# Eight leading matmuls, the cross-attention's output product in seven block products, and an issue order written as a table

## The chip, the core and the metric

The kernel runs on one core of one Trainium2 chip. The number that counts is the device time of one execution in microseconds (us), as a median of several runs. Five engines work side by side on a core, each through its own queue in order: TensorE (PE in the profile; its weight loads are PEld), VectorE (DVE), ScalarE (ACT), GpSimd (POOL) and SyncE (SP), which here issues most of the DMA transfers.

## What is computed

Two encoder layers over 512 positions of width 1024, all in float32. Each has a mixing part (differential attention beside a recurrent branch), a cross-attention into 256 memory tokens, and an MLP; every part ends in a matrix product that is added to the residual `x`. Cut to what matters here:

```
for l in range(DEPTH):                              # DEPTH = 2
    h = rms_norm(x, g_mix[l]);  z = h @ w_in[l]
    ...                                             # attention o, recurrent branch r
    x = x + concatenate([o, r]) @ w_out[l]
    hq = rms_norm(x, g_xq[l])
    qx = (hq @ xa_wq[l]).reshape(B, S, X_HEADS, X_HEAD_DIM)     # 4 heads of 256
    ...
    p = softmax(einsum('bshd,bmhd->bhsm', qx, kx) * X_HEAD_DIM ** -0.5)
    ox = einsum('bhsm,bmhd->bshd', p, vx).reshape(B, S, D_MODEL)
    x = x + ox @ xa_wo[l]                           # the product that is changed
    hm = rms_norm(x, g_mlp[l])
    x = x + square(relu(hm @ mlp_w1[l])) @ mlp_w2[l]
return rms_norm(x, g_final)
```

## The kernel before

**Layout and precision.** `x` lies transposed: eight chunks `c_x` of 128 channels by 512 positions. To keep float32 accuracy every operand of a product is split into a rounded part and a rest (`hi` and `lo`, by one ScalarE copy and one VectorE subtraction), and each product is three matmuls: hi by hi, hi by lo, lo by hi. A weight tile is 128 by 1024 floats, so 512 KB: SyncE loads it into `wraw` (three buffers), ScalarE makes `whi`, VectorE `wlo` (three buffers each). In the profile all work of the program has one line, L490, since one helper (`emit`) issues it; groups are told apart by tile names: `b` is any 128 by 512 work tile, `mm` (three) and `at` (five) are PSUM banks, `s` small columns, `pt` the transposed attention probabilities and some scratch.

**The order.** `trunk` writes the whole program down as operations in a `Plan` (`record`); `schedule` then places them by an estimate of each one's duration, due times and a string of corrections (`LEADS`), and `emit` issues them in that order. So what stands behind what on an engine is fixed when the program is built.

**The start.** GpSimd fills constants, among them `c_ones` and the identity. SyncE and ScalarE load parameters, `x` and the first weights, in halves. ScalarE and VectorE split the first chunk and the first weight half, and then TensorE begins `v_products`: 96 matmuls of 512 columns, chunk after chunk. A small product of `c_ones` (`lam_col`) stands in front of them.

**The cross-attention's end.** For each of four heads (`XHead`): scores, softmax, transposition (`turn`), and `pv`, which makes two tiles of 128 by 512 and splits each in hi and lo (list `ox`, eight tiles). Then `residual_fm` is called eight times a layer: `gemm_fm` multiplies one weight tile with the eight chunks (24 matmuls of 128 by 128 by 512), and VectorE adds the result to `x[c]`. `prep_x` scales and splits the new chunk for the MLP.

**The MLP's second product** is already done otherwise. `left_pair` turns two neighbouring tiles into the seven left operands of a 2 by 2 block product in seven multiplications, `right_pair` turns two weight tiles into the seven right operands, and `seven` does the seven products. Each product is 12 matmuls of 256 columns, and its bank is added to the residual in one or two pieces of 128 by 256.

Of the kernel before, what the change touches and what calls it, by code (L numbers as in the profile page):

```python
# [11 lines left out]
F32 = mybir.dt.float32  # L12
# [6 lines left out]
P = 128  # L19
# [30 lines left out]
ATT_AHEAD = 3  # L50
SPLIT_AHEAD = 18.0
LOAD_AHEAD = 105.0
CAST_AHEAD = 28.0
NEG_AHEAD = 20.0
DMA_T = (1, 4, 13, 36, 51)


LEAD_STEPS = '#$%&()*+,-./0123456789:;<=>?@ABCDEFGHIJKLMNOPQRSTUVWXYZ[]^_`abcdefghijklmnopqrstu'
LEADS = (
    'uL63BCuGGgGGGG@@<<HGuue>d>auFOMu9Q-ZAAGA-2D-H)?NNOC*@%AD?EA#6&/,0,?CBBB,=5>BBDFA?1J1C-G;JF$80?FUFKP;'  # L60
    'eOD?AK9NLPBWOOZ``Y[S^YcRURQTTRQNPLNNNTJJPIJJLISQR[XMMXXOGHOJFMMABIQPVUkUU[[[WTPSSLLJLuuLRSCNRJJJKJEG'
    'GVSXQNMECF>lK`LLJIJIKKNK```KCDDIDcCjL[YSeY_Ua0^NGLLGGLIGP>LEU@@D@0L4HHKKPutukM<=tYfYfBKOPKuuuu[uTZuK'
    'JOOHTtmqtmufuuFCVbmuDDM7MRLCZrruuu0&u?;;;K6CDC4uuuuuuCuuuuMussuguuuuKIDQa>OEYC;>X@<EgqlsultlllutluPQ'
    'QVV:Wqo^^ZQQF25BGIuuuuuuuuuuNZknIBNEKiWuuuuuuuuuutuusGGA:LJGN_quU_lYYYVuuuuuubuuuubuuuudsuuu_lonEbab'
    'QkdkGWhmmS^E_aetGFV`UmiusL7U1UaaUoOJJkVV`N_MJCEEGRFHHHRKFMDLJJKJ@@@MDMJCHDNHHGHHHRGPHKOOHGOHHHVHLAIP'
    'KKKTLTTHHHI6IL>CCRI:RI5JLJV@HPGH;JC;>IGKHDFFCFHFHCFBBBAB@@HIOED_RLLQLEREHEHISTWVTH`VLLJLLMILGLLLMP_^'
    'LLLWUL^LOHJPXLrRWRffVRLPJOOLAPPPNKP_QOFOLOIWFWYMPW]RLRRLLLLLLLLLVLULLULLULLLLLLLLLLVLQSUNLLLELCLILLH'
    'TOOPOO[OOGA@IA@A@KKIKGIKGMIGGILNKJLRPQLLLKKLJLLOLRLLMJLKLLLLLILKKLHHHCH8I8HI8HHHLLI8LLILLLLLLI8LSSSS'
    'SLL8I8L8ILJIJJJLCJLMJLLPLLHLOLLKNLLLLCLALK>LLLLLK<LH>LLLLLK>LLQNN@GQLGKLLNMLQQLPNKKLPJJLKHLVL[LL>RIJ'
    'LLMEOFFGFEW5VU2[VWF$ZZ#W#KG)JDHDFJQ#n]5U^Ru:ufaX`7b2X5pCbGdYQ_RRVAF[Ac[]qsqnoqrPgXHdS=g5LkBTOKGG_?Gu'  # L70
    '<GJIIAbMUASrUMqMb`L`MTMMMMNNNXeZ_ZndVOTTMZMZdeghZZXUMZZZZZZZUUUYUKZSZ[bbbbeeKeJiIK^J]]XUVNQQ=R=IFFJL'
    'LNKKKKWKLJOLLNMLMNLOONNLOLLNNLLONNLLLLOOMONONQLLQMLCLOOOLLSLLMONLONSNLLLLLHLMLFFFILMOLNLFFILNHGLLLLK'
    'LNLMMKLLNLNNLXMLXLLXMLLNLLLMLMXNLLYLLMXLNLMLIXXHLHLLLLHXXHHLIXDLLLLKLLLDUFLQDKQLFELLILCCCFCOEKBBDPEE'
# [12 lines left out]
    'uuutkhbbbusinVTYofODlQ@7lOTGodhkMUjajDTMGgh`JLHZ5QG9m/2:6OR888D;;dZCERCCCEGE@<@:B@:::B@G?>>G>;CCDCCH'
    'G>NPNN@RUTB5B;5?;<;7;;B8;B;8BBFGIAII@>>;><99>>>9>9H?>GGGGGGNMB7D7>ABRMHHOKA?G@GBGJCBNBMBJE=B[NcNcEEd'
    'O?aREEuuuuuuuuWJuu[eH;u;R36Lcm/JHPA?M2Y:IWYt`PPPuPPRQUPPSPVIccicPcce]Rubl[RPHVL@VEXXuuDSluJNKSSQuPPP'
    'NPPSTQ_bnf^WXWRWoJGERPAPBPWL]ZG?QITFGLPHRJcGY]hYWJdNbPUPZgUTf_XZZ_uY[[SZ[u`n_bZHRRJegaXFD[>[=^3_SS1V'
    'LIEiQH-S2$tnneC^ReSNGHH>H7><;THHEHMHHB>P=C@HOFTQDLHeHQdOVUUMMYWY_jQYeeXMMMM_eMMMMMKMKK_bMKKKKaaVVVLQ'  # L90
    'WcWLdLWLSLXNNPPPRQPPP[P_WP[RSP[PE[[[[____GCGPPP[WPWWPPPVVPPRPPD>BCPJWPPOPPPPPCURCO=SXPYSRQIIINIIXV^Q'
    '``SFSPEDAAEELRWTZdMIMNMSSTSOTUOd^WV[XLJLLOLLJ]]ORUUGQFO[MGGGGGGFF*#WaUYa[DSbJLhLoK<UMEKL4UCJa0X/U*%&'
    '[###M###M%%+FOurMuuuruA.mP(S888?=EKHUT_M*MMPLSiuQlaJouuB*=Auuuuuuuuquusu777VAu@qQXWFUXZ.-5=AAEEE???D'
    'T-Z2uuuuuuuuusZZXjTTIHmuumuuuuuIGXGDSAL[Hu`YWURQEHMLHZZ[uuuZuuuuutQuuuuHuouoKuouILS_RJIXYQVV]G^fIPZP'
    'Tu]gXNWuuuuq[agLOmtm;iRULYbe]]]]g[VMOLGUKLNPLOLLLHNLNOOG@WJXLYP`fkGUZHGIPLJLEJJODP@@jluuuuSNchaY^LQE'
    'SIIEAEAOOjJ<<56JCJCBME>8AQTAI<VINOGNLIG[1B83E49>FfNl=>?>?NNDCDLI4QNNIK=EHON0:5=7G^uA5c9UDZAT+=G9GFEG'
    'FEIJJJAOOOL(KMOMP#T;L<L;D:DBM3M@H1*6?9<FiiCJH,GI]cQKZRT`<QLHWV]be_uuuZLRULBBIIQTUSIZWK`LJQQLLEL]IXRI'
# [1465 lines left out]
```

## Time and profile before

| | |
|---|---|
| median of three runs | 1463.85 us (1462.7 to 1465.16) |
| the profiled execution, its own time | 1463.46 us |
| its span in the trace | 1461.7 us |
| TensorE busy | 1430.8 us, 98% of the span |
| VectorE busy | 1108.0 us, 76% |
| ScalarE busy | 758.2 us, 52% |
| chain that ended last | TensorE 82%, VectorE 10%, DMA 3%, ScalarE 3% |

Busy times are unions, so two pipelined matmuls that overlap count once. An engine's share of the whole span says little about one stage; tables by stretch (busy time of each engine between two times, with the number of instructions in it) and the waits of TensorE, with who ended each, say more. For the pace of matmuls the distance from one start to the next is used, not the duration of one, since they overlap.

### The profile page before, as it was taken

Reading aid. Unit: us, or ns where it says so; the run is one execution under the profiler, and the core shown is the slowest. Engines: PE = TensorE matmul, PEld = TensorE weight load, DVE = VectorE, ACT = ScalarE, POOL = GpSimd, SP = SyncE. Lnnn points to the kernel's source line nnn. Section 1 sums busy time; section 2 is a strip of 40 time slices with the busy share of each in tenths; the row PEclk is TensorE's granted clock in tenths of the full one; section 3 lists DMA queues with packets and bytes.
Section 4 is the critical chain, followed back from the end, with each engine's and each line's share of the span. In section 5 each row is a group of like instructions: output and inputs, shape, how many; then the busy total and the mean of one; then the engine's idle time right before and its main releaser. Section 6 shows DMA issues by size and latency. Waiting matters only on the chain.

```text
span 1461.7 us, 20808 instructions
## 1 busy us (share of the span) xinstructions
PE 1430.8 (98%) x8054; PEld 1228.4 (84%) x8054; DVE 1108.0 (76%) x1891; ACT 758.2 (52%) x1164; POOL 41.5 (3%) x69
## 2 busy tenths in 40 slices
PE   8999999999999999999999999999999999999997
PEld 6777887888889889898987779888888898989986
DVE  7889886564679697797958999755655786959786
ACT  6598755443445353444536887644443544435352
POOL 1000000000000000000000011000000000000001
PEclk9999999999999999999999999999999999999998
DMA  6454643221323233233334565422122233232322
GB/s 204 116 144 106 183 159 90 98 72 38 108 87 102 101 102 101 101 102 101 101 115 113 145 167 166 132 87 87 59 71 87 101 102 115 74 115 90 119 81 72
DMA packets 50258, 157.67 MB, mean 108 GB/s; under 512 B 6384, under 2 KB 8560, under 8 KB 50160
## 3 DMA queue, kind: packets, MB, share of 16 engines
q1 hardware_dynamic: 47136, 145.61, 31.1%
q0 software_dynamic: 2880, 10.49, 3.4%
q8 instruction: 63, 1.03, 0.3%
q14 instruction: 35, 0.29, 0.1%
q10 hardware_dynamic: 144, 0.26, 0.0%
HBM read 141.65 MB, written 2.10 MB: 98 GB/s over the span
## 4 chain that ended last, share of the span: by engine, by line
PE 82%; DVE 10%; DMA 3%; ACT 3%; issue 1%; POOL 0%; SPq 0%; DVEq 0%; ACTq 0%; POOLq 0%
PE mm L490 63%; PE at L490 18%; DVE b L490 6%; DVE wlo L490 2%; ACT b L490 1%; DVE s L490 1%; DMA b<-b 1%; DMA wlo<-in_W 1%; ACT whi L490 1%; DVE pt L490 1%; DMA whi<-in_W 1%; DMA wraw<-in_W 0%; ACT L490 0%; POOL s L490 0%; SPq L490 0%
## 5 line engine op out<-in xcount | busy, mean ns | idle before, releaser
L490 PE MATMUL mm<-b,whi 128*128 128x512 f32 (+1 forms) x3640 | 976.4, 356 | 2.5 <-DVE b L490 1.7
L490 PEld LDWEIGHTS mm<-b,whi 128*128 128x128 f32 x3640 | 632.7, 188 | 107.6 <-ACT b L490 3.2
L490 PE MATMUL mm<-b,wlo 128*128 128x512 f32 (+1 forms) x1820 | 645.5, 355 | 1.7 <-DVE wlo L490 1.6
L490 ACT ACTIVATE whi<-wraw 128x1024 fp32r<-128x1024 f32 (+1 forms) x213 | 223.1, 1048 | 346.3 <-PE mm L490 186.8
L490 PEld LDWEIGHTS mm<-b,wlo 128*128 128x128 f32 x1820 | 342.3, 188 | 56.9 <-DVE wlo L490 2.8
L490 DVE TENSOR_TENSOR wlo<-wraw,whi 128x1024 fp32r<-128x1024 f32 (+1 forms) x213 | 257.1, 1208 | 41.3 <-ACT whi L490 40.3
L490 DVE TENSOR_TENSOR b<-b,b 128x512 fp32r<-128x512 f32 (+3 forms) x388 | 223.0, 594 | 10.1 <-ACT b L490 8.6
L490 ACT ACTIVATE b<-b 128x512 fp32r<-128x512 f32 (+2 forms) x288 | 168.8, 602 | 80.7 <-DVE b L490 78.0
L490 DVE SCALAR_TENSOR_TENSOR b<-mm,rb 128x512 f32<-128x512 f32 x80 | 55.2, 690 | 106.5 <-PE mm L490 105.7
L490 DVE TENSOR_TENSOR c_x<-c_x,mm 128x256 f32<-128x256 f32 (+1 forms) x160 | 74.5, 471 | 72.5 <-PE mm L490 71.9
L490 ACT ACTIVATE whi<-pt 128x1024 fp32r<-128x1024 f32 x64 | 67.6, 1060 | 98.9 <-PE mm L490 41.8
L490 PE MATMUL at<-b,whi 128*128 128x256 f32 x520 | 94.6, 278 | 0.0
L490 ACT ACTIVATE b<-at,s 128x512 f32<-128x512 f32 (+2 forms) x100 | 61.1, 615 | 45.6 <-DVE s L490 37.4
L490 PEld LDWEIGHTS at<-b,whi 128*128 128x128 f32 x520 | 79.6, 188 | 0.9
L490 DVE TENSOR_TENSOR wlo<-pt,whi 128x1024 fp32r<-128x1024 f32 x64 | 77.9, 1221 | 2.9 <-ACT whi L490 2.7
L490 PE MATMUL at<-b,wlo 128*128 128x256 f32 x260 | 72.4, 278 | 0.1
L490 PE MATMUL at<-b,b 128*128 128x256 f32 (+1 forms) x320 | 65.7, 331 | 4.7 <-DMA b<-b 3.9
L490 DVE TENSOR_REDUCE s<-at 128x1 f32<-128x512 f32 (+1 forms) x80 | 54.6, 687 | 16.8 <-PE at L490 16.6
L490 PEld LDWEIGHTS at<-b,b 128*128 128x128 f32 x320 | 47.4, 190 | 12.7 <-DMA b<-b 4.8
L490 PE MATMUL at<-b,pt 128*128 128x256 f32 x384 | 53.8, 278 | 0.0
L490 PE MATMUL at<-pt,b 128*128 128x256 f32 (+1 forms) x288 | 50.0, 319 | 2.2 <-DVE pt L490 2.2
L490 DVE TENSOR_TENSOR c_x<-c_x,at 128x256 f32<-128x256 f32 x97 | 39.5, 417 | 13.9 <-PE at L490 13.4
(127 smaller groups left out, 1234.8 us busy)
## 6 DMA issues: line engine op xcount, KB each, us to landing
wraw<-in_W SPq DMA_DIRECT2D x239, 512.0 KB, 3.3
b<-b SPq DMA_DIRECT2D x96, 128.0 KB, 2.5
whi<-in_W POOLq DMA_DIRECT2D x10, 512.0 KB, 4.0
wlo<-in_W POOLq DMA_DIRECT2D x10, 512.0 KB, 5.5
wraw<-in_memT SPq DMA_DIRECT2D x4, 512.0 KB, 5.4
out_T<-b SPq DMA_DIRECT2D x16, 128.0 KB, 1.8
c_x<-in_xT SPq DMA_DIRECT2D x7, 256.0 KB, 6.2
wraw<-in_W SPq DMA_DIRECT2D x6, 256.0 KB, 4.5
```

The costliest lines, as they stand in the source:

```text
L490: getattr(self.engines[op.eng], m)(*a, **k)
```

## The change

Three things are changed.

1. Eight matmuls of `c_ones` by `c_ones` (128 columns, plain float32) are put in front of the program. Their result is used by nothing.
2. The cross-attention's output product is done by `seven`, as the MLP's second product is. `pv` no longer splits its two tiles; it copies the first out of PSUM and calls `left_pair`. The eight calls of `residual_fm` a layer become four of `seven`.
3. `schedule` and its estimates are gone. The order is a table of 6276 numbers (`ISSUE`), two characters each, which says which operation stands at each place; `order` reads it. The table covers all engines, and hardly a stretch of the program keeps its old order.

```diff
+WARM = 8
-LEADS = (
-    'uL63BCuGGgGGGG@@<<HGuue>d>auFOMu9Q-ZAAGA-2D-H)?NNOC*@%AD?EA#6&/,0,?CBBB,=5>BBDFA?1J1C-G;JF$80?FUFKP;'
...
+ISSUE = (
+    '#-###=#+#.#,#1#$#/#%#&%r%s&+$v#(#*%*#>%+#9#;#D#:#A#@#C#B#<#E#K#I#0$:$;$<#5#L#M#J#H#3#2#4%,#P$=#Q#a#e'
...
-    def schedule(self):
...
+    def order(self):
+
+        at = [DIGITS.index(a) * 90 + DIGITS.index(z) for a, z in zip(ISSUE[::2], ISSUE[1::2])]
+        assert sorted(at) == list(range(len(self.ops)))
+        place = {self.ops[i]: p for p, i in enumerate(at)}
+        for op in self.ops:
+            assert all(place[p] < place[op] for p in op.preds | op.behind if p is not op)
+        return sorted(self.ops, key=place.get)
...
+    warm = AT()
+    with plan.group():
+        for _ in range(WARM):
+            PE.matmul(warm[:, :P], ones, ones, start=True, stop=True)
...
-                hi, lo = R(), R()
-                split(hi, lo, pm)
-                out.append((hi, lo))
-            return out
+                out.append(pm)
+            te = T()
+            A.activation(te, out[0], AF.Copy)
+            return left_pair(te, out[1])
...
-            ox += hd.pv()
+            ox.append(hd.pv())
         nrm = Norm()
         xs = [None] * KD
-        for m in range(8):
-            residual_fm(l, T_XO + m, ox, m)
-            xs[m] = prep_x(l, "g_mlp", m, nrm)
+        for m in range(0, 8, 2):
+            seven(l, T_XO + m, T_XO + m + 1, ox, m, m + 1)
+            for c in (m, m + 1):
+                xs[c] = prep_x(l, "g_mlp", c, nrm)
```

Two places of the order are shown, the start and the first layer's last cross-attention head. The number behind a name is that of the instruction which wrote the tile. TensorE at the start of the program, before (`at_107` is the small product of `lam_col`, the rows behind it are `v_products`):

```order
L490 MATMUL at_107<-s_97,c_ones_76 128x2
L490 MATMUL mm_133<-whi_119,b_101 128x512
L490 MATMUL mm_133<-wlo_127,b_101 128x512
L490 MATMUL mm_133<-whi_119,b_121 128x512
L490 MATMUL at_144<-whi_119,b_101 128x512
```

and now:

```order
L391 MATMUL at_97<-c_ones_95 128x128 x8
L391 MATMUL at_110<-s_106,c_ones_95 128x2
L391 MATMUL mm_119<-whi_112,b_70 128x512
L391 MATMUL mm_119<-wlo_117,b_70 128x512
L391 MATMUL mm_119<-whi_112,b_108 128x512
```

The eight new matmuls need `c_ones` alone and stand first. The constants on GpSimd, before (`xb` and `b` are tiles that are zeroed ahead of their use):

```order
L490 MEMSET c_mhalf_68 128x4
L490 MEMSET c_ones_76 128x128
L490 MEMSET b_78 128x512
L490 MEMSET c_ident_83 128x128
L490 MEMSET xb_85 128x2
L490 ISA
L490 AFFINE_SELECT c_ident_83<-c_ident_83 128x128
```

and now:

```order
L391 MEMSET c_ident_83 128x128
L391 ISA
L391 AFFINE_SELECT c_ident_83<-c_ident_83 128x128
L391 MEMSET xb_88 128x2 x2
L391 MEMSET xb_91 128x2
L391 MEMSET b_93 128x512
L391 MEMSET c_ones_95 128x128
```

`c_ones` has moved from the second place to the last of these. ScalarE's first work has moved too: the split of `x0` and both halves of the first weight stand ahead of the squares of `x0`, which stood first.

VectorE in layer 0, behind the last head's softmax, before (`pt_3495` the rests of the transposed probabilities, `b_3527` and `b_3538` the rests of `pv`'s two tiles, `c_x_0_66` the first chunk of the residual):

```order
L490 TENSOR_TENSOR pt_3495<-at_3479,pt_3489 128x2x256
L490 TENSOR_TENSOR pt_3495<-at_3484,pt_3489 128x2x256
L490 TENSOR_TENSOR b_3527<-at_3511,b_3522 128x512
L490 TENSOR_TENSOR b_3538<-at_3518,b_3532 128x512
L490 TENSOR_TENSOR c_x_0_66<-c_x_0_66,mm_3420 128x512
L490 TENSOR_TENSOR wlo_3560<-wraw_3252,whi_3552 128x1024
L490 SCALAR_TENSOR_TENSOR b_3570<-c_x_0_66,c_prm_70,b_3558 128x512
```

and now (rows on `at_3466` and `b_3497` are the third head's `left_pair`, those on `at_3554` and `b_3571` the fourth's; `wlo_3563` and `pt_3582` are the second weight pair):

```order
L391 TENSOR_TENSOR b_3504<-b_3504,b_3497 128x256
L391 TENSOR_TENSOR b_3541<-b_3497 128x256
L391 TENSOR_TENSOR pt_3535<-at_3515,pt_3533 128x2x256
L391 TENSOR_TENSOR b_3544<-at_3466,b_3538 128x512
L391 TENSOR_TENSOR b_3541<-at_3466,b_3504 128x256
L391 TENSOR_TENSOR wlo_3563<-wraw_3302,whi_3461 128x1024
L391 TENSOR_TENSOR b_3565<-b_3541,b_3561 128x512
L391 TENSOR_TENSOR b_3579<-b_3571 128x256
L391 TENSOR_TENSOR b_3573<-b_3571,b_3573 128x256
L391 TENSOR_TENSOR pt_3582<-wraw_3302,wraw_3567 128x512
L391 TENSOR_TENSOR b_3584<-b_3571,at_3554 128x256
L391 TENSOR_TENSOR b_3606<-at_3554,b_3577 128x512
```

Where two subtractions stood between `pv` and the first addition to the residual, the left operands of two heads and the right operands of the second weight pair are now interleaved. TensorE at the same place, before: the end of `pv`, then products that use the weights of chunk 1 and 2 while the last head is split:

```order
L490 MATMUL at_3518<-pt_3489,b_2524 128x512
L490 MATMUL mm_3491<-b_3409,whi_3347 128x512
L490 MATMUL mm_3491<-b_3418,whi_3347 128x512
L490 MATMUL mm_3491<-b_3409,wlo_3359 128x512
L490 MATMUL mm_3534<-b_3089,whi_3390 128x512
L490 MATMUL mm_3534<-b_3104,whi_3390 128x512
```

and now:

```order
L391 MATMUL at_3554<-pt_3533,b_2811 128x512
L391 MATMUL at_3586<-b_3263,whi_3461 128x256
L391 MATMUL at_3586<-b_3269,whi_3461 128x256
L391 MATMUL at_3586<-b_3263,wlo_3563 128x256
L391 MATMUL at_3586<-b_3349,whi_3461 128x256
L391 MATMUL at_3586<-b_3351,whi_3461 128x256
L391 MATMUL at_3586<-b_3349,wlo_3563 128x256
L391 MATMUL mm_3416<-b_3573,whi_3267 128x256 x2
L391 MATMUL mm_3416<-b_3573,wlo_3329 128x256
```

The terms of the first three heads are multiplied with two weight pairs before the fourth head's first operand (`b_3573`) is asked for.

## Rows read from the trace of the kernel before

**Rows 1.** The page: busy time of each engine, share of the span, instructions

```profile
PE 1430.8 (98%) x8054; PEld 1228.4 (84%) x8054; DVE 1108.0 (76%) x1891; ACT 758.2 (52%) x1164; POOL 41.5 (3%) x69
```

**Rows 2.** Busy time by stretch, with instructions (x), TensorE clock, DMA share, GB/s

```profile
0.00:12.00 12.00, 6.59 (x18) 4.96 (x19) 6.72 (x18) 8.53 (x15) 1.95 (x14) 1.00 0.83 284
50.00:230.00 180.00, 171.30 (x912) 142.26 (x911) 159.78 (x283) 135.97 (x230) 11.29 (x21) 0.99 0.52 142
230.00:690.00 460.00, 460.00 (x2574) 396.57 (x2573) 324.37 (x518) 200.15 (x295) 3.04 (x3) 1.00 0.28 92
750.00:950.00 200.00, 195.05 (x1051) 163.70 (x1050) 175.02 (x310) 147.98 (x239) 15.62 (x19) 1.00 0.51 143
1405.00:1462.00 57.00, 45.98 (x373) 43.81 (x371) 42.15 (x80) 20.48 (x30) 4.21 (x6) 0.91 0.20 65
```

**Rows 3.** TensorE's waits by releaser (us in total, times, longest), first and last of twelve

```profile
PE at L490 <- DVE s L490: 5.6, 3, 4.2
...
PE mm L490 <- DVE c_x L490: 0.2, 1, 0.2
```

**Rows 4.** Chain that ended last, in time order (start, us, what), product and first layer MLP

```profile
1072.05 42.00 PE mm L490 x180
```

**Rows 5.** Busy time by stretch, cross-attention and MLP of layer 0

```profile
270.00:395.00 125.00, 125.00 (x608) 103.53 (x607) 71.78 (x112) 50.57 (x94) 1.01 (x1) 1.00 0.23 76
320.00:395.00 75.00, 75.00 (x356) 61.80 (x355) 42.17 (x64) 30.37 (x54) 0.00 (x0) 1.00 0.22 77
455.00:486.00 31.00, 31.00 (x273) 31.00 (x272) 27.93 (x49) 13.48 (x16) 0.00 (x0) 1.00 0.31 103
623.00:659.00 36.00, 36.00 (x303) 35.36 (x302) 32.20 (x56) 14.00 (x17) 0.00 (x0) 1.00 0.31 103
692.00:730.00 38.00, 37.00 (x311) 35.90 (x310) 37.30 (x64) 21.37 (x28) 0.00 (x0) 1.00 0.27 90
```

**Rows 6.** VectorE groups by shape (count | busy us, mean ns | idle before, releaser)

```profile
L490 DVE TENSOR_TENSOR wlo<-wraw,whi 128x1024 fp32r<-128x1024 f32 x207 | 253.0, 1223 | 40.8 <-ACT whi L490 39.8
L490 DVE TENSOR_TENSOR c_x<-c_x,mm 128x256 f32<-128x256 f32 x128 | 52.6, 417 | 20.3 <-PE mm L490 19.7
L490 DVE TENSOR_TENSOR pt<-wraw,wraw 128x512 f32<-128x512 f32 x32 | 22.0, 686 | 0.6 <-DMA wraw<-in_W 0.6
L490 DVE TENSOR_TENSOR c_x<-c_x,mm 128x512 f32<-128x512 f32 x32 | 22.0, 686 | 52.3 <-PE mm L490 52.2
L490 DVE TENSOR_TENSOR b<-at,b 128x512 fp32r<-128x512 f32 x16 | 11.0, 691 | 9.9 <-ACT b L490 9.7
```

**Rows 7.** TensorE in time order at the start (start, us, instruction)

```profile
4.17 0.56 PE L490 MATMUL at<-s,c_ones 128*128 128x2 f32 x2 [4.17 <-DVE s L490]
5.96 0.80 PE L490 MATMUL mm<-whi,b 128*128 128x512 f32 x1 [1.23 <-ACT whi L490]
...
7.74 0.63 PE L490 MATMUL at<-whi,b 128*128 128x512 f32 x1
...
10.73 0.41 PE L490 MATMUL mm<-wlo,b 128*128 128x512 f32 x1
```

**Rows 8.** GpSimd in time order at the start

```profile
0.77 0.20 POOL L490 MEMSET c_ones<- 128x128 f32 x1
0.91 0.53 POOL L490 MEMSET b<- 128x512 f32 x1
...
1.66 0.29 POOL L490 TENSOR_SCALAR_AFFINE_SELECT c_ident<-c_ident 128x128 f32<-128x128 f32 x1
```

**Rows 9.** ScalarE in time order at the start

```profile
4.58 0.71 ACT L490 ACTIVATE b<-c_x,c_prm 128x512 fp32r<-128x512 f32 x1
...
5.30 0.61 ACT L490 ACTIVATE whi<-wraw 128x512 fp32r<-128x512 f32 x1
```

**Rows 10.** Busy time by stretch, a long wait and the time behind it

```profile
160.00:166.00 6.00, 3.99 (x30) 3.45 (x29) 6.00 (x15) 5.97 (x13) 0.00 (x0) 1.00 0.60 150
168.00:171.00 3.00, 3.00 (x16) 3.00 (x16) 3.00 (x10) 0.68 (x3) 1.59 (x2) 0.50 0.89 306
```

More of the change, by code (lines that the diff above doesn't have):

```diff
@@ L203, in __init__ @@
         self.tag, self.shape, self.dtype, self.name = tag, list(shape), dtype, name
-        self.log, self.left, self.tile, self.slot, self.end = [], 0, None, None, 0.0
+        self.log, self.tile = [], None
 class _Op:
-    __slots__ = ("eng", "calls", "dur", "key", "idx", "npred", "succ", "ready", "roots", "new",
-                 "table", "start", "end", "bytes", "preds", "behind")
+    __slots__ = ("eng", "calls", "dur", "idx", "roots", "preds", "behind")
 class _Engine:
@@ L302, in record @@
             op.eng, op.calls, op.dur, op.idx = eng, [], 0.0, len(self.ops)
-            op.succ, op.roots, op.new, op.ready, op.preds, op.behind = {}, [], [], 0.0, set(), set()
-            op.table, op.bytes = None, 0
-            op.key = self.t - self.lead
+            op.roots, op.preds, op.behind = [], set(), set()
             self.ops.append(op)
@@ L554, in weight_dma @@
         src = W[l * NT + t]
-        with plan.ahead(CAST_AHEAD):
-            G.dma_start(out=hi, in_=src)
-        with plan.ahead(NEG_AHEAD):
-            A.activation(lo, b(hi), AF.Copy, scale=-1.0)
-            G.dma_start(out=lo, in_=src, accum_op=ALU.add)
+        G.dma_start(out=hi, in_=src)
+        A.activation(lo, b(hi), AF.Copy, scale=-1.0)
+        G.dma_start(out=lo, in_=src, accum_op=ALU.add)
         return hi, lo
@@ L570, in weight @@
         lo = plan.tile("wlo", [P, 1024], F32R)
-        with plan.ahead(SPLIT_AHEAD):
-            for cs in (slice(0, 512), slice(512, 1024)) if first else (slice(0, 1024),):
-                split(hi[:, cs], lo[:, cs], raw[:, cs])
+        for cs in (slice(0, 512), slice(512, 1024)) if first else (slice(0, 1024),):
+            split(hi[:, cs], lo[:, cs], raw[:, cs])
         return hi, lo
@@ L601, in trunk @@
     prm = C([P, NPAR], F32, "prm")
-    with plan.ahead(1000.0):
-        SP.dma_start(out=prm, in_=par)
+    SP.dma_start(out=prm, in_=par)
     post = C([P, 4], I32, "post")
@@ L607, in load_x @@
     def load_x(c, q):
-        with plan.ahead(900.0 - c):
-            q.dma_start(out=x[c], in_=xT[c * P:(c + 1) * P, :])
+        q.dma_start(out=x[c], in_=xT[c * P:(c + 1) * P, :])
     def pc(l, name, i):
@@ L1144, in mem_load @@
             m = plan.tile("wraw", [P, 1024], F32)
-            with plan.ahead(LOAD_AHEAD):
-                SP.dma_start(out=m, in_=memT[:, 1024 * i:1024 * (i + 1)])
+            SP.dma_start(out=m, in_=memT[:, 1024 * i:1024 * (i + 1)])
             out.append(m)
@@ L1410, in trunk @@
         while todo:
-            with plan.ahead(ATT_AHEAD):
-                step()
+            step()
         while fill(100.0):
```

399 lines of the change are left out of this document (148 added, 251 removed).

## The prediction

> **What bounds the kernel now.** I read the page's busy times first: TensorE is busy for 1430.8 us of the span of 1461.7, VectorE for 1108.0 and ScalarE for 758.2 [rows 1]. So TensorE's own work is the bound, and two things can be won: less work there, or part of its 30.9 idle us. The table by stretch says where these lie [rows 2]: 5.4 in the first 12 us (6.59 busy of 12), 8.7 in the mixing part of layer 0 (171.30 of 180), none at all from 230 to 690, 4.95 in the second mixing part, 11.0 in the last 57. In the mixing parts VectorE is at 159.78 of 180 and 175.02 of 200, the nearest to a second bound. TensorE's waits agree: twelve kinds, 22.6 us together, the largest 5.6 in three waits and the smallest 0.2 [rows 3]; no single wait is worth much. In the cross-attention and the MLP nothing but the number and pace of matmuls counts, as long as VectorE and ScalarE deliver in time.
>
> **The output product of the cross-attention.** Removed: two layers of 8 x 24 = 192 matmuls of 512 columns, 384 in all. The pace is read from the chain of waits: 180 matmuls in a row in 42.00 us, 0.2333 each [rows 4], so 89.6 us for 384.
>
> Added: two layers of 4 x 7 x 12 = 336 matmuls of 256 columns, 672 in all. Their pace is read in the MLP's second product, which has this form already: 31 us hold 273 matmuls (0.1136 each), 36 hold 303 (0.1188), 38 hold 311 (0.1222) [rows 5]. 672 of them come to 76.3, 79.8 or 82.1 us. I take the middle one, since eight blocks of the old kernel's own seven-product MLP lie around it; the third has VectorE at 37.30 of 38 and stands for a stretch that VectorE slows. **The term: 89.6 - 79.8 = 9.8 us less**, with ends 13.3 and 7.5.
>
> **What pays for it.** VectorE, each layer: removed are eight weight rests at 1.223, eight additions of 512 columns at 0.686 and eight splits of `pv`'s tiles at 0.691, 20.8 us [rows 6]. Added are, for each of four weight pairs, three rests of 128 by 1024 (two weights are split as they are, others are sums of halves), five additions or subtractions of 128 by 512 at 0.686 and about seven updates of 256 columns at 0.417: 3.7 + 3.4 + 2.9 = 10.0; and for each head's `left_pair` five sums of 256 columns at 0.417 and three rests at 0.691, 4.2. Four of each are 56.8, so 36 us more a layer. That is the change's real price and it is off the path only if there is room. There is: from 320 to 395 (last heads and the product itself) VectorE is busy 42.17 of 75, from 270 to 395 it is 71.78 of 125 [rows 5]. With 36 more the shorter stretch, which would take about 70, would need 78 and overflow by 8; the longer, about 120, needs 108 and holds it. So it comes down to whether the new order draws the work ahead into the query product. It does in part: the rests and sums of the first weight pairs and of the first three heads stand before the last head's, and TensorE has the products of three heads with two weight pairs to run before it asks for the fourth's first operand. Between the fourth head's softmax tail and that operand I count twelve VectorE rows worth about 7.2 us against 6.6 to 7.4 us of matmuls queued ahead: near balance, a wait of a microsecond at most. I add nothing for it and keep up to 4 us a layer as a bound, the overflow of 8 being what could happen if nothing were drawn ahead. ScalarE gains some 13 us a layer and is at 30.37 of 75 there [rows 5]: covered. The weights come with the same transfers in the same number, so the DMA load does not change.
>
> **The leading matmuls.** Before, TensorE's first product starts at 5.96, and its first ten matmuls of 512 columns take until 10.73, 4.77 us, or 0.43 from start to start where the steady ones read 0.57, 0.23 and 0.23 further down [rows 7] and 0.2333 in the chain [rows 4]. 512 columns in 0.43 us is the lower level of the clock, 1.2 GHz, although the clock column shows 1.00 for these 12 us [rows 2]. At full pace the ten would take 2.35, so **2.4 us is the most that can be won**. Ahead of them stood only the two short records of `lam_col` at 4.17 [rows 7].
>
> Now eight plain float32 matmuls go first. One such product leaves two records (the `x2` at 4.17), so 16. Each costs between a quarter of 0.43 (128 of 512 columns: 0.107) and the 0.28 of `lam_col`'s records: 1.7 to 4.5 us, an estimate; I take 0.21 and 3.4. They wait for `c_ones`. Its fill was GpSimd's second instruction (0.77, 0.20 us); now it stands behind the identity (whose selection ended at 1.95), three small tiles and a fill of 512 columns (0.53) [rows 8], so I put it at about 2.1 us. The eight then end at 5.5 and `lam_col` at about 5.95. The first product's operands: ScalarE now splits `x0` first and then the weight, which used to end at 5.91 behind the square and the split of `x0` (4.58 and 5.30) [rows 9]; without the square ahead they could be there by about 5.3. So the start stays at 5.9 to 6.0: operands are earlier, the queue of TensorE isn't. What is won is pace. 3.4 + 0.45 us of work stand where ten half-pace matmuls went by before the pace rose, as much time as nine of those; then one or two remain slow, and the ten take about 2.7 instead of 4.77. **The term: 2.0 us less.** Bounds: if the eight take 4.5 the product starts 1.1 later and wins 1.3 net; if the clock does not heed them, nothing is won and up to 0.6 is lost (the first product held up by TensorE's queue); at best 2.4.
>
> By the Trainium skill (TensorE: Matmul & The Clock Gate, Part 1, "What's actually happening") the number of slow matmuls at the start of one and the same kernel differs from run to run (6, 11 or 14 are named). If that held here the gain would be anything between nothing and the 2.4, and not the same in each run; the one profiled execution of before, with its ten, cannot show a spread.
>
> **The order.** The table moves rows on every engine in every stage, and neither gains nor loses by its nature. What it can win lies in the mixing parts: 8.7 and 4.95 us of idle [rows 2], and the 3 us behind the longest gap of layer 0, where TensorE had 3.99 busy of 6 and then ran 3 us at a granted 0.50 [rows 10], 1.5 us. What it can lose is of the same kind: VectorE there is at 89% and 88%, and an order that is a little worse turns its queue into waits. I take **0**, from -7 (half of these waits go) to +6 (half as much again comes). The last 57 us keep their instructions and I leave them as they are.
>
> **Rivals.**
> - *The order also removes waits.* Half of the 13.65 us and of the 1.5 go, 7 more: 1444.7. For it: VectorE and TensorE rows of the mixing parts are interleaved anew throughout. Against it: with VectorE near 90% little can be moved.
> - *The leading matmuls do not bring the pace forward.* The ten stay at 0.43, and the sum is 1463.46 - 9.8 + up to 0.6, so about 1454. It needs no fault elsewhere, only that what these matmuls do is too little to raise the clock, or that it falls again in the gap before the first product. The skill's spread, above, bears on this case.
> - *The cover at the last head fails.* TensorE waits some 4 us a layer for the fourth head's left operands or a late weight pair: 1451.7 + 8 = 1460.
> - *Slower than before.* VectorE's added 36 us are not drawn ahead: its queue overflows by 8 us in each layer [rows 5], 16 together, and TensorE comes out of each wait at half clock as it did behind the gap of layer 0 [rows 10]: 1451.7 + 16 + 1 to 2 = 1469. It decides from waits of 11.7 us over both layers. Against it: I saw the first three heads' work standing ahead in the order.
> - *That the change doesn't do what it says* can only be the case for the leading matmuls, and is the second rival.
>
> **How the numbers follow.** The profiled execution took 1463.46, the median is 1463.85 (1462.7 to 1465.16); they agree within 0.4, so the sum goes against 1463.46: 1463.46 - 9.8 - 2.0 + 0 = **1451.7, so 1452**. Chances: forecast (1447 to 1456.5) 0.55; waits removed too (about 1445) 0.17; no gain in pace (1454) 0.10; cover fails (about 1460) 0.12; slower (1469) 0.06. The range leaves out the slower case, part of the failing cover and the deepest of the gains: 1443 to 1460. A measurement of this kernel tells about 0.2% from no change, 2.9 us, so faster means below 1460.9: all of the first three cases and half of the fourth, 0.88; within, 0.06; slower, 0.06.
>
> **What would show it.** In the changed profile: TensorE's busy time down by about 8 (9.8 and 2.0 less, the leading 3.4 more) and VectorE's up by some 72 (36 a layer); the seven blocks of the output product at 0.114 to 0.122 a matmul, with less than 2 us of waits at the fourth head in each layer; 16 short records from about 2 us on, the first product near 5.95, and at most two of its matmuls at 0.43; the idle time of the mixing parts near 13.65 us together. Wrong would be: ten slow matmuls as before (the second term falls), a wait for VectorE's left or right operands of several us (the cover), blocks at over 0.13, or idle time in the mixing parts that differs by more than 7 us from before, which would mean that the order, and not the two edits, set the time.

## The result: 21 us less, where 12 were forecast

| | before | changed |
|---|---|---|
| median | 1463.28 us (4 runs beside the changed kernel) | 1441.94 us (1441.38 to 1444.45) |
| ratio | 1 | 0.9858, 95% interval 0.984 to 0.9875 |
| the profiled execution, its own time | 1463.46 us | 1441.38 us |
| its span | 1461.7 us | 1439.6 us |

The sign was forecast, the size was not: 1441.94 lies below the range (1443 to 1460). Of the terms of the sum the product was right, the leading matmuls were worth less than half of what was set down, and the order, set at nothing, was worth as much as the product.

The page of the changed kernel, busy times (answers to [rows 1]):

```profile
PE 1419.9 (99%) x8358; PEld 1238.2 (86%) x8358; DVE 1157.9 (80%) x2027; ACT 771.4 (54%) x1201; POOL 44.1 (3%) x69
```

TensorE is busy 10.9 us less and idle 11.2 us less (19.7 instead of 30.9). That is not half work and half waiting: 2.9 us of this idle time, in the first 12 us, are only filled by the leading matmuls, whose 3.8 us stand in the busy time. The table by stretch of the changed kernel (answers to [rows 2]; columns as there) says where the waiting went:

```profile
0.00:12.00 12.00, 9.48 (x33) 7.96 (x34) 5.18 (x12) 6.49 (x11) 1.47 (x12) 1.00 0.81 279
50.00:230.00 180.00, 176.57 (x965) 149.22 (x964) 163.79 (x296) 139.86 (x234) 15.12 (x23) 1.00 0.53 148
230.00:690.00 460.00, 459.65 (x2772) 404.84 (x2771) 356.06 (x597) 211.77 (x321) 3.31 (x2) 1.00 0.27 92
750.00:950.00 200.00, 197.77 (x1058) 166.38 (x1057) 176.65 (x302) 145.57 (x236) 12.60 (x17) 1.00 0.50 142
```

The idle time of the two mixing parts fell from 8.7 to 3.4 and from 4.95 to 2.2 us, 8.0 together. In the same 180 us TensorE now runs 965 instructions where it ran 912. VectorE is a little busier in both, since the same work stands closer together: at 89% and 88% it was not the bound that it looked like.

The waits of TensorE in the changed kernel (answers to [rows 3]), the first three and the last of nine:

```profile
PE at L391 <- DVE b L391: 2.5, 4, 1.7
PE at L391 <- POOL s L391: 2.1, 1, 2.1
PE at L391 <- POOL c_mhalf L391: 2.1, 1, 2.1
...
PE mm L391 <- DVE c_x L391: 0.2, 1, 0.2
```

Two kinds are gone: those for a small column from VectorE (5.6 us before [rows 3], of which 4.2 was the time before TensorE's first record), and those for transfers of rotated halves, which before were:

```profile
PE at L490 <- DMA b<-b: 3.9, 4, 1.7
```

The 2.1 for `c_mhalf` is the time before the first leading matmul.

### The profile page after: what moved, and what is told of

It reads as the page before. It is cut to its first block, busy times and chain, and to the rows that moved or that the text cites. A ratio compares the mean times of both kernels' runs of the same rounds, so it can differ in the third digit from the quotient of the medians.

```text
span 1439.6 us, 21603 instructions
## 1 busy us (share of the span) xinstructions
PE 1419.9 (99%) x8358; PEld 1238.2 (86%) x8358; DVE 1157.9 (80%) x2027; ACT 771.4 (54%) x1201; POOL 44.1 (3%) x69
## 4 chain that ended last, share of the span: by engine, by line
PE 81%; DVE 5%; DMA 1%; issue 1%; ACT 1%; POOL 0%; DVEq 0%; ACTq 0%; POOLq 0%
PE mm L391 61%; PE at L391 20%; DVE b L391 4%; DMA wlo<-in_W 1%; DVE s L391 1%; DVE wlo L391 1%; DVE pt L391 1%; ACT b L391 0%; DMA wraw<-in_W 0%; POOL s L391 0%; ACT whi L391 0%; ACT pt L391 0%; ACT wlo L391 0%; DVE c_x L391 0%; ACT rb L391 0%
## 5 line engine op out<-in xcount | busy, mean ns | idle before, releaser
L391 PE MATMUL mm<-b,whi 128*128 128x512 f32 (+1 forms) x3640 | 944.4, 348 | 1.3 <-ACT b L391 1.0
L391 DVE TENSOR_TENSOR b<-b,b 128x512 fp32r<-128x512 f32 (+3 forms) x420 | 241.2, 590 | 18.1 <-ACT b L391 14.3
L391 PE MATMUL at<-b,whi 128*128 128x256 f32 x648 | 120.9, 279 | 0.0
L391 DVE TENSOR_TENSOR wlo<-pt,whi 128x1024 fp32r<-128x1024 f32 x80 | 97.5, 1220 | 6.0 <-ACT whi L391 5.1
L391 PEld LDWEIGHTS at<-b,whi 128*128 128x128 f32 x648 | 100.4, 189 | 2.1
L391 PE MATMUL at<-b,wlo 128*128 128x256 f32 x324 | 90.3, 279 | 0.0
L391 PE MATMUL at<-b,pt 128*128 128x256 f32 x480 | 73.2, 279 | 0.0
L391 PEld LDWEIGHTS at<-b,pt 128*128 128x128 f32 x480 | 64.5, 188 | 1.6
L391 DVE TENSOR_REDUCE s<-at 128x1 f32<-128x512 f32 (+1 forms) x80 | 54.1, 683 | 11.0 <-PE at L391 10.9
L391 PEld LDWEIGHTS at<-b,wlo 128*128 128x128 f32 x324 | 60.9, 188 | 0.0
L391 DVE TENSOR_TENSOR pt<-pt,wraw 128x512 f32<-128x512 f32 x80 | 54.9, 686 | 0.3
```

The source lines that it names most:

```text
L391: getattr(self.engines[op.eng], m)(*a, **k)
```

## The experiments

Twelve kernels were run, each beside the kernel before. Where only the order differs, "the new order" means the table of the changed kernel and "the old order" what the planner of the kernel before gave; instructions that one of them does not have were placed by TensorE's progress. "Mended" means that around the seams, or around the output product, places were then searched anew, one instruction at a time, keeping what shortened TensorE's estimated waits.

| label | product | order | leading matmuls | median us | ratio to before, 95% |
|---|---|---|---|---|---|
| changed | new | new | yes | 1441.9 | 0.984 to 0.9875 |
| e1_old_product | old | new, unmended | yes | 1465.4 | 0.9998 to 1.0021 |
| e5_old_product2 | old | new, mended | yes | 1452.8 | 0.9906 to 0.9937 |
| e2_new_product | new | old, unmended | no | 1540.1 | 1.0504 to 1.0541 |
| e6_new_product2 | new | old, mended | no | 1457.8 | 0.9947 to 0.9975 |
| e3_mix_old | new | old in both mixing parts, unmended | yes | 1473.4 | 1.0046 to 1.0083 |
| e8_mix0_old | new | old in layer 0's mixing part | yes | 1453.0 | 0.9902 to 0.9939 |
| e12_mix1_old | new | old in layer 1's mixing part | yes | 1450.5 | 0.9881 to 0.9917 |
| e11_mix0_new | old | old, new in layer 0's mixing part | no | 1458.8 | 0.9951 to 0.9976 |
| e7_scores_later | old | old, sixteen score steps moved | no | 1472.0 | 1.0041 to 1.0069 |
| e4_no_lead | new | new | no | 1443.7 | 0.9833 to 0.987 |
| e9_early_start | new | new, start earlier | yes | 1440.9 | 0.983 to 0.9857 |
| e10_early_no_lead | new | new, start earlier | no | 1444.3 | 0.9846 to 0.9879 |

### The product and the order, apart

**e1_old_product and e5_old_product2.** Both keep the new order and go back to the old product:

```diff
-            te = T()
-            A.activation(te, out[0], AF.Copy)
-            return left_pair(te, out[1])
+                hi, lo = R(), R()
+                split(hi, lo, pm)
+                out.append((hi, lo))
+            return out
...
-        for m in range(0, 8, 2):
-            seven(l, T_XO + m, T_XO + m + 1, ox, m, m + 1)
+        for m in range(8):
+            residual_fm(l, T_XO + m, ox, m)
```

> The new order and the eight leading matmuls, with the output product of the cross-attention in its old form (384 matmuls of 512 columns). Theory A (the two gains add: the product is worth what its own matmuls save, 10 us, and the order is worth another 10 in the mixing parts): 1452, TensorE's busy time up by about 10 against the changed kernel, idle in 50 to 230 and 750 to 950 us still 3.4 and 2.2 us. Rival B (the order's gain hangs on the new product, as room it left): 1458 to 1463, with the idle of the mixing parts back at 8 and 5. Rival C (the product is worth nearly all 21 us by what it does to its neighbours): 1461 or more with unchanged idle in the mixing parts.

It took 1465.4, as long as rival C wanted, but not for its reason. The idle time of the mixing parts stayed low (TensorE busy 176.16 of 180 and 197.82 of 200), and adding up the distances from matmul to matmul by stage shows 5.4 and 4.5 us more in the cross-attention's scores of the two layers, with single waits up to 3.1 us; the new order had been made for other work there than the old product has. So the run could not decide, and it was mended.

> As the first try of the old product in the new order (with the leading matmuls), but with the instructions between the query product and the first MLP products placed anew for the old product, so that the last head does not wait for what was meant for another product; the mixing parts and the rest keep the new order. Theory A (gains add): 1452 to 1454, that is the changed kernel plus the 10 to 11.5 us that the product's own matmuls are longer; waits of the last head's scores below 2 us a layer where the first try had 5. Rival B (the order's gain hangs on the new product): 1458 or more though these waits are gone.

1452.8: theory A. By the same adding up, the old product takes 45.1 and 45.6 us here, the new one 39.9 and 40.6 in the changed kernel: 10.1 us for both layers, and 10.9 between the two medians. The table by stretch of this run, the mixing parts:

```profile
50.00:230.00 180.00, 176.26 (x963) 149.03 (x962) 164.03 (x295) 139.74 (x234) 14.85 (x23) 1.00 0.54 148
750.00:950.00 200.00, 197.84 (x1063) 166.61 (x1062) 176.65 (x302) 144.75 (x237) 11.43 (x17) 1.00 0.51 142
```

TensorE's and VectorE's busy times are those of the changed kernel within 0.4 us. So with the old product the order (with the leading matmuls, which won nothing in this run's profile, see The start) is worth 1463.5 - 1452.8 = 10.7 us. It needs no room left by the product.

**e2_new_product and e6_new_product2.** The other way round, the new product in the old order (the code is that of the changed kernel with the lines of `WARM` left out; only the table differs):

> The old order, without the leading matmuls; only the output product in its new form, its instructions put among the old ones where the new order has them by TensorE's progress. Theory A (gains add): 1453, idle in the mixing parts 8.7 and 5 us as before, the product about 79 us for both layers. Rival B: 1445 or less. Rival D (VectorE's added 36 us a layer need the new order to be hidden): above 1457, with waits of TensorE for VectorE's operands between 330 and 395 us and about 720 us later.

1540 us, 76 slower than before. This is the prediction's rival "slower than before", larger than it was priced: by the same adding up, layer 0's product took 78.6 us where the changed kernel has 39.9, and layer 1's 63.6 where that has 40.6. The run's waits of TensorE from 320 to 460 us:

```profile
PE at L391 <- DVE b L391: 12.1, 5, 4.9
PE at L391 <- ACT whi L391: 9.3, 2, 8.3
PE mm L391 <- ACT whi L391: 8.2, 2, 7.2
```

VectorE was busy for only 59.75 of the 100 us from 320 to 420, so it is not its load that did it. Weights that ScalarE had to split, and operands from VectorE, stood in their queues behind work that itself waited, and TensorE ran 74 of these 100 us at a mean granted clock of 0.89. The prediction's test, added work against room, does not see this: what counts is where the work stands.

> The old order in the mixing parts and the MLP, no leading matmuls; the output product in its new form, with the stretch from the query product to it in the new order and its seams placed anew. Theory A (gains add): 1453, product at about 79 us for both layers together, idle in 50 to 230 us and 200 us of layer 1's mixing part as before (8.7 and 5). Rival D (VectorE's added work is hidden only where the whole order is new): 1458 or more with waits of over 4 us a layer at the product; the first try, with VectorE's work in the old places, had some 39 and 27 us of them.

1457.8, between A (1453) and D (1458 and up). The products took 39.2 and 40.0 us, as they should; the mixing parts kept their old idle time (171.33 busy of 180); but the cross-attention's own stages gave back 1.3 us (scores of layer 0), 1.3 (transpositions of both layers) and 1.2 (`pv` of both). So the cover is not free in an order that was not made for it, and the two gains do not simply add: 10.9 in the new order, 5.7 in the old.

### Where the order's gain sits

**e8_mix0_old, e12_mix1_old, e3_mix_old, e11_mix0_new.** Only rows of the table change. In e12_mix1_old this is more than its label says: some 300 places of layer 0, run from 223 to 313 us (the end of its mixing part and its query products), differ from the changed kernel too. TensorE ahead of the first scores of layer 0 in e8_mix0_old (their operands are the rotated halves that transfers have just brought):

```
L392 MATMUL at_636<-b_606,b_542 128x512
L392 MATMUL at_636<-b_593,b_542 128x512
L392 MATMUL at_644<-b_606,b_542 128x512
```

They begin at 55.3 us there; in the changed kernel 21 more matmuls stand ahead of the first scores, which begin at 60.2 us.

> The changed kernel, with the instructions of both mixing parts (and of the memory keys and values) put back in the order that they had before among themselves; all else as changed. Theory A (the order's gain is the mixing parts' waits): 1451 to 1453, idle in 50 to 230 and 750 to 950 us back at about 8.7 and 5 us, stretches at granted clock 0.5 come back. Rival E (the order's gain lies elsewhere, in the MLP or the end): 1442 to 1445.

> The changed kernel with only the mixing part of layer 0 in its old order. Theory A: up by what that part lost before, 6 to 8 us, to 1448 to 1450; idle in 50 to 230 us back at 8.7, in 750 to 950 still 2.2. Rival E (the earlier try's loss came from its seams and not from the mixing part): 1442 to 1444.

> The changed kernel with only the mixing part of layer 1 in its old order, its two seams placed anew. Theory A: by the starts of its matmuls that part lost 2.6 us to the new order in the two profiles, so 1444 to 1446, with idle in 750 to 950 us back at about 5 (2.2 in the changed kernel) and waits for the transfers of the rotated halves back at 2.5 us; idle in 50 to 230 us still 3.4. Rival I (the old order there costs as much as that of layer 0 did, 11 us): 1450 or more.

The first of them (1473.4) lost 15 us in the mixing parts and 9 more at the seam to the query products, so its total says little; its idle time says what was expected (9.6 and 5.2). The mended ones: with layer 0's old order the kernel takes 11 us more (1453.0), with layer 1's 8.5 (1450.5; its profiled execution took 1454.0). Both are above what was expected, and 1450.5 is the number of rival I; where these microseconds lie is told below. In e8_mix0_old, then e12_mix1_old, the mixing parts and what follows a long wait:

```profile
50.00:230.00 180.00, 169.77 (x906) 140.18 (x905) 159.62 (x281) 135.38 (x228) 12.01 (x22) 1.00 0.52 141
228.00:231.00 3.00, 2.46 (x6) 1.98 (x7) 0.48 (x1) 0.69 (x1) 0.00 (x0) 0.57 0.03 11
750.00:950.00 200.00, 197.83 (x1064) 166.81 (x1064) 175.41 (x309) 145.86 (x237) 13.27 (x18) 1.00 0.51 140
```

```profile
50.00:230.00 180.00, 174.40 (x951) 147.35 (x950) 162.49 (x291) 139.77 (x234) 14.59 (x21) 1.00 0.53 146
750.00:950.00 200.00, 195.47 (x1037) 164.00 (x1036) 175.62 (x302) 146.64 (x236) 12.63 (x17) 0.99 0.50 140
821.00:824.00 3.00, 3.00 (x12) 2.52 (x11) 2.65 (x5) 2.06 (x5) 0.00 (x0) 0.59 0.00 0
```

Where the old order stands, idle time of 10.2 and 4.5 us stands too, and 3 us at a granted clock of 0.57 or 0.59 behind a wait, as [rows 10] had it: in e12_mix1_old behind 1.9 us for a rotated half, in e8_mix0_old behind 2.7 us for a weight's transfer to `wlo`, at a seam (1.6 us at the same place before, 0.8 in the changed kernel). Cut into pieces of 3 us, the mixing parts have one or two below 0.9 in the kernel before, e2, e3, e6, e7, e8, e11 and e12, and none in the changed kernel, e1, e4, e5, e9 and e10, which have the new order in both. In e11 these pieces stand in the part that has the new order, behind the wait told next, so the new order is not safe from them. Where it avoids a wait it wins twice: the wait, and the slower matmuls behind it.

> The kernel before (old product, no leading matmuls) with only the mixing part of layer 0 in the new order, and the seam to the query product placed anew. Theory A: the reverse of the run that put it back, so 8 to 11 us less than before, 1453 to 1456; idle in 50 to 230 us at 3.4 to 4, in 750 to 950 still about 5. Rival H (the gain of that part needs the other edits): 1459 or more.

1458.8, between the two: 5.6 us won where e8_mix0_old lost 11. Its profiled execution (1465.2, the longest of six) shows one reason. ScalarE and TensorE of that run:

```profile
140.10 0.91 ACT L386 ACTIVATE b<-wraw,c_prm 128x256 fp32r<-128x256 f32 x2 [3.77 <-DMA wraw<-in_memT]
```

```profile
145.57 0.89 PE L386 MATMUL at<-c_ident,b 128*128 128x128 f32 x4 [3.19 <-ACT b L386]
```

The new order lets ScalarE stand at a transfer of memory tokens. In the changed kernel's trace it stood there 2.0 us and TensorE noticed nothing; here 3.8, and in e4_no_lead and e12_mix1_old 4.2, and TensorE waited 3.2, 1.4 and 1.4 us for what was queued behind it. That place has no slack, and the landing of one transfer decides it. How much of the difference between 5.6 and 11 this explains was not settled.

The traces say where the losses of the three runs lie. Two stretches, cut by the starts of matmuls: from the 30th matmul of `v_products` to the last of layer 0's output product of the mixing part, and from the last of layer 0's MLP to the last of layer 1's output product of the mixing part:

| one profile each, us | layer 0's stretch | layer 1's stretch |
|---|---|---|
| before | 262.6 | 252.8 |
| changed | 253.0 | 248.3 |
| e5_old_product2 | 253.1 | 248.2 |
| e8_mix0_old | 268.3 | 247.9 |
| e12_mix1_old | 255.4 | 253.2 |
| e11_mix0_new | 259.3 | 252.9 |

In the two mixing parts the new order wins some 9.5 and 4.5 us, with either product; the old product's run gives some of these 14 us back in other stages, which leaves 10.1 in its profile. Layer 1's old order costs 4.9 us where it stands. The rest of what e12's profile lost (12.5 us) lies elsewhere: 2.4 us in layer 0, ahead of the places that differ there and with TensorE's wait behind the memory tokens, 2.6 in layer 1's cross-attention behind the seam, 2.1 in the last MLP. Layer 0's old order, put back in e8, takes 5.7 us longer than it took before, with the long wait at its seam; 3.7 us of that come back in the cross-attention that follows.

**e7_scores_later.** The old kernel, with the score steps of two heads in each layer moved back by four TensorE operations. Since neighbouring steps move along, the first of them gets three matmuls of other work ahead of it, far fewer than the 21 of the new order. Around it, before and now:

```
L490 MATMUL mm_578<-b_274,wlo_511 128x512
L490 MATMUL at_629<-b_599,b_535 128x512
L490 MATMUL at_629<-b_586,b_535 128x512
```

```
L386 MATMUL mm_578<-b_274,wlo_511 128x512
L386 MATMUL mm_635<-b_101,whi_533 128x512
L386 MATMUL mm_635<-b_121,whi_533 128x512
L386 MATMUL mm_635<-b_101,wlo_548 128x512
L386 MATMUL at_643<-b_599,b_535 128x512
```

> The kernel before, with only the score products of the first two heads of both layers moved back by four TensorE operations each, so that other matmuls stand between the transfers of the rotated halves and the products that read them. Theory F (a good part of the order's gain is such a distance): the waits of these products for transfers, 3.9 us before, fall below 1.5, and the time to about 1460. Rival G (the wait only moves to the next operation): 1463 to 1464, with as much idle time in 50 to 230 us as before, 8.7.

1472.0, 8.5 slower than before: neither theory. The waits of TensorE in this run:

```profile
PE mm L386 <- ACT b L386: 4.3, 7, 1.2
PE at L386 <- DVE pt L386: 4.0, 3, 1.5
...
PE at L386 <- DMA b<-b: 0.5, 1, 0.5
```

Theory F's mechanism held (the waits for transfers went from 3.9 to 0.5 us), and its conclusion fell. TensorE now waits for what ScalarE makes (4.3 us in seven waits, six of them of gate products), and `pv` for the probabilities; that the exponentials, which come later on ScalarE's queue, hold this up is argued from the order and not shown. Curing this one wait alone brought others; the new table moved all engines' rows together.

### The start

**e4_no_lead.** The group is left out, the rest of the table is kept.

```diff
-    warm = AT()
-    with plan.group():
-        for _ in range(WARM):
-            PE.matmul(warm[:, :P], ones, ones, start=True, stop=True)
```

> The changed kernel without the eight leading matmuls. Theory A (they did not bring the pace forward: in the profiles of before and after the rise comes at 10.7 and 10.5 us alike): 1441.5 to 1442, the first product at about 5.9 instead of 6.44, the step from 0.43 to 0.23 us a matmul again near 10.6 us. The prediction's step (they are worth 2 us): 1444, with ten or more matmuls at 0.43 us and the rise after 11 us.

1443.7 against 1441.9, with ratios whose intervals overlap nearly whole: the time cannot tell. The traces can, since every run has a start. The start of TensorE's first product, the number of slow matmuls behind it (0.43 us or a wait apart, until they come 0.23 apart) and the start of the 30th:

| no leading matmuls | first | slow | 30th | leading matmuls | first | slow | 30th |
|---|---|---|---|---|---|---|---|
| before | 5.96 | 10 | 15.11 | changed | 6.44 | 9 | 15.37 |
| e2 | 5.99 | 13 | 15.68 | e1 | 6.55 | 2 | 13.96 |
| e4 | 6.49 | 10 | 15.78 | e3 | 6.01 | 2 | 13.30 |
| e6 | 5.91 | 13 | 15.66 | e5 | 6.50 | 9 | 15.60 |
| e7 | 5.90 | 12 | 15.42 | e8 | 5.90 | 9 | 14.69 |
| e10 | 5.49 | 7 | 14.00 | e9 | 5.40 | 8 | 14.08 |
| e11 | 6.51 | 13 | 16.38 | e12 | 6.46 | 10 | 15.58 |

Without: 7 to 13 slow ones, 11 in the mean; with: 2 to 10, 7 in the mean. The 30th starts 0.8 us earlier in the mean (14.65 against 15.43). These 0.8 us hang on two profiles: in e1 and e3, with two slow matmuls, the way from the first to the 30th took 7.4 and 7.3 us, against 9.15 before; in the other five it took 8.7 to 9.1, against 8.5 to 9.9 in the seven without. So the eight can bring the pace forward by nearly the predicted 2.0 us, and did in two profiles of seven; one profile of each kernel does not fix the mean. In the profile of the changed kernel itself they won nothing. Nor did they hold the start up: without them, in e4_no_lead, the first product came at 6.49 and not near 5.9, as had been expected. The Trainium skill (TensorE: Matmul & The Clock Gate, Part 1, "What's actually happening") says that the number of slow matmuls at the start differs from run to run of one kernel. No kernel has two profiles here; as far as they go the traces agree, with 2, 9, 9 and 10 for four kernels that start alike (e1, changed, e5, e12).

**e9_early_start and e10_early_no_lead.** The first product came at 6.44, not at the 5.95 of the prediction. TensorE and ScalarE of the changed kernel:

```profile
2.09 3.78 PE L391 MATMUL at<-c_ones 128*128 128x128 f32 x16 [2.09 <-POOL c_mhalf L391]
5.66 0.42 PE L391 MATMUL at<-s,c_ones 128*128 128x2 f32 x2
6.44 0.79 PE L391 MATMUL mm<-whi,b 128*128 128x512 f32 x1 [0.36 <-ACT whi L391]
```

```profile
3.85 1.28 ACT L391 ACT_TABLE_LOAD   x1 [3.85 <-DMA c_prm<-in_par]
5.15 0.72 ACT L391 ACTIVATE b<-c_x,c_prm 128x512 fp32r<-128x512 f32 x1
```

ScalarE's load of its function table stands in front of its first computation and here waits for what that one waits for, the parameters. Before, it ran at 1.18:

```profile
1.18 1.28 ACT L490 ACT_TABLE_LOAD   x1 [1.18 <-PEq L1558]
4.04 0.63 ACT L490 ACTIVATE b<-c_x 128x512 f32<-128x512 f32 x1 [1.58 <-DMA c_x<-in_xT]
```

There the first computation was the square of `x0`, which needs `x0` alone; it waited for that transfer with the load already done. Now the first computation is the split, which needs `x0` and the parameters, and the load waits for the parameters too. The square, which the prediction was glad to be rid of in front of the split, had cost some 0.5 us (the split came at 4.58 [rows 9], and at 4.02 in e9_early_start below, which has neither the square nor the late load), but it had the load done early. The two runs give ScalarE a first computation without a transfer, and fill the ones first (by the table):

```diff
+    A.activation(C([P, 1], F32, "tiny"), ones[:, 0:1], AF.Copy)
```

> The changed kernel with an earlier start: the ones are filled by GpSimd's first instruction, and ScalarE gets a first instruction that needs only them (128 by 1), so that the load of its function table no longer stands behind the parameters' transfer. Expected: table load at about 1.2 us instead of 3.85, leading matmuls from about 1.0 to 4.8, first product at about 5.3 instead of 6.44; 1440 to 1441 if only that 1.1 us is won, 1438 to 1440 if the pace rises earlier too. Against it: the leading matmuls end before the first product and leave a gap, so that the pace rises no earlier than in the kernel without them.

> The kernel with the earlier start, without the leading matmuls. If these are worth what they were meant for, the step from 0.43 to 0.23 us a matmul comes 2 to 4 us later than in the one with them and the time is 1 to 2 us longer; if not, both are within 0.5 us and the step comes between 10 and 12 us in both.

In e9_early_start:

```profile
1.18 1.28 ACT L392 ACT_TABLE_LOAD   x1 [1.18 <-PEq L1455]
2.47 0.20 ACT L392 ACTIVATE c_tiny<-c_ones 128x1 f32<-128x1 f32 x1
4.02 0.72 ACT L392 ACTIVATE b<-c_x,c_prm 128x512 fp32r<-128x512 f32 x1 [1.35 <-DMA c_x<-in_xT]
```

The split of `x0` comes 1.1 us earlier and the first product at 5.40 (5.49 without the leading matmuls). 1440.9 is the lowest median of all kernels here, but its interval overlaps the changed kernel's: a gain of 1 us that the trace shows and the clock of the whole run cannot. Between e9 and e10 lie 3.4 us in the medians, more than either case expected, while in the two profiles the 30th matmul starts at 14.08 and 14.00; so that difference is not the leading matmuls' doing, as far as these profiles go.

## Why the prediction was wrong, step by step

- **The product, 9.8 us: right.** By stage sums 10.1 (e5 against changed), by medians 10.9. The chosen pace of 0.1188 was near: in the changed kernel, inside the product of layer 0, and the old product in e5_old_product2:

```profile
344.00:376.00 32.00, 32.00 (x273) 31.84 (x271) 30.97 (x55) 15.64 (x20) 0.00 (x0) 1.00 0.21 72
```

```profile
351.00:385.00 34.00, 34.00 (x147) 27.27 (x146) 17.03 (x21) 14.93 (x20) 0.00 (x0) 1.00 0.27 89
```

  32 us hold 273 matmuls, 0.1172 each; 34 hold 147, 0.2313 each. VectorE went from half busy to 97% of the stretch.
- **VectorE's price, 72 us: right as a sum of durations, too high as busy time; its cover: right for this order.** With the same number of instructions added (136), the durations rose by 69.0 us from e5_old_product2 to the changed kernel, and VectorE's busy time by 56.5 (from 1101.4): an addition of 512 columns is 0.69 us long, while the next in VectorE's queue starts 0.60 after it, so that neighbours overlap. The new order did draw the work ahead: scores, transpositions and `pv` of the cross-attention took only 0.5 and 0.9 us more than before in the two layers. e2 and e6 show that another order hides it in part or not at all, which the prediction's balance of work and room could not show.
- **The leading matmuls, 2.0 us: about 0.8 in the mean of seven profiles a side, none in the profiled execution.** What was forecast came in two profiles of seven, so the sum took for certain what one execution may or may not give. Its bound of 2.4 was too wide as well: the first two matmuls stood 0.8 to 0.9 and 0.3 us ahead of their followers even at the fast pace (e1, e3), and the most that any profile won on the way to the 30th is 1.9 us. That the first product could start at 5.95 failed at ScalarE's table load.
- **The order, 0 (between -7 and +6): this is the step that failed.** It was worth 10.7 us with the old product (e5, the leading matmuls included). The prediction's own sign of it came: the idle time of the mixing parts was to be near 13.65, a difference of more than 7 would mean that the order set the time, and it is 5.7. The prediction knew the pieces, 13.65 us of idle in the mixing parts and 1.5 behind a wait, and held half of them for the most that it would win, with the argument that VectorE near 90% leaves little to move. The measured 8.0 us of idle are 59% of it, the 1.5 went too (no piece of 3 us in the mixing parts is below 0.9 any more), and VectorE simply became busier (159.78 to 163.79 of 180). Besides, the idle column understates each wait: a matmul of 512 columns is drawn as 0.39 us long and the next may start after 0.23, so up to 0.16 us of every wait is covered by the record before it; with twenty starts in the mixing parts that came over 0.25 us late before and ten now, that is an estimated 1.6 us of gain that no idle time shows.
- **The rival "the order also removes waits" was the case that came**, at 0.17, priced at 7 where 10.7 were due. All of the idle time and of the 1.5 would have priced it at 15.2 and the time at 1436.5, so the measured 1441.9 lies between half of them and all.

What stays open: the parts of the order do not add. Put back alone, layer 0's part costs 11.0 and layer 1's 8.5, together more than the 10.7 that the whole order is worth with the old product; brought in alone, layer 0's wins 5.6. By the stretches above, some 3.6 of the 8.5 lie outside layer 1's mixing part, and 5.7 us of layer 0's stretch in e8 are more than the old order itself had. These stretches come from one profile of each kernel; which share is seams that were mended by hand, and which is the landing time of single transfers, the runs do not tell.

## What to carry to other kernels

Where an issue order is replaced as a whole, take all of the idle time and of the half-speed stretches behind it for its bound, not half of them: here some 11 of 15 us were won. A busy share of 88% on a second engine does not say that the waits for it must stay. Added work on a second engine is covered or not by its place in the queues, not by the sum of free time: the same instructions made the kernel 5.7 us faster or 76 slower. And a wait that is cured by moving one engine's rows can come back on another queue, as in e7_scores_later, so look at the next two waits before pricing the first.

## What the runs showed of the hardware

- ScalarE's first function table load (1.28 us) stands just ahead of its first computation. It ran at 1.18 us before, where that computation needed one transfer and itself waited 1.58 us for it, and at 3.85 in the changed kernel, where the computation needed two transfers and the load waited for one of them. A computation of 128 by 1 on a constant in front moved it back to 1.18.
- Between two computations a table load cost about 1.3 us: in all 29 loads of the kernel before after the first one, the next computation began 1.29 us after the load's start.
- Additions of 128 by 512 in a row on VectorE are 0.69 us long each and start 0.60 us apart.
- Eight plain float32 matmuls of 128 columns make 16 records and took 3.78 us in the changed kernel, 0.24 each.
- The number of slow matmuls at the start was 2, 9, 9 and 10 in kernels that start alike (e1, changed, e5, e12).
- A 512 KB transfer of memory tokens in the same place of the program kept ScalarE 1.6 to 4.2 us in seven of the eight profiles with the new order in layer 0.
